# Two chains in the mixers: S5 moved behind RWKV and into its PSUM banks, RG-LRU left behind sparse attention

## The chip, the core and the metric

One core of a Trainium2 chip runs the whole program. The metric is the device time of one execution in microseconds (us), and lower is better. TensorE is called PE here, VectorE DVE, ScalarE ACT, GpSimd POOL, and SP is the queue that issues the weight transfers.

## What is computed

The program is a decoder trunk of two layers over 256 tokens, 1024 wide, in float32. In each layer the normalized input is projected once, and four causal token mixers, each 256 wide, work on parts of that projection. Their outputs are projected back to 1024, weighted by sigmoid gates and summed, and a mixture of experts follows.

```python
h = rmsnorm(x, mix_norm_g[l]) * (1.0 + scale1) + shift1
u, q, k, v, iq, ik, iw, rg_x, rg_g, rw_f = _split(h @ w_in[l], IN_WIDTHS)
o_s5 = s5_mixer(u, ...)          # diagonal complex state space scan, gelu, GLU
o_dsa = dsa_mixer(q, k, v, iq, ik, iw, positions)   # indexer, top 64 keys, attention
o_rg = rglru_mixer(rg_x, rg_g, ...)   # width 4 convolution, gates, real scan, gelu gate
o_rw = rwkv7_mixer(rw_f, ...)    # token shift, delta rule recurrence, group norm, bonus, gate
up = einsum('btnw,nwd->btnd', [o_s5, o_dsa, o_rg, o_rw], branch_w[l])
gates = sigmoid(h @ gate_w[l] + gate_b[l])
x = x + gate1 * ((gates * up).sum(branches) @ out_w[l])
x = x + gate2 * moe(rmsnorm(x, ffn_norm_g[l]) * (1.0 + scale2) + shift2)
```

## The kernel before, in words

The four mixers are Python generators. Each `yield` ends a piece of work, and a loop at the end of the program (L1741 to L1748) takes one piece from each chain in turn. The order of those pieces, and a scheduler behind it that keeps each engine's instructions in one queue, set what stands where. Nothing in that order depends on run time. Each engine works through its own queue in order.

The kernel before has two long chains. The first is `rwkv` (from L787): projections, the products of one chunk of 64 tokens with another, five levels of a triangular inverse (L944 to L957), a recurrence over four chunks (L963 to L1000), then a normalization of each head (L1003 to L1012, L1020) that has to be transposed back through PE (L1014). The second is `others` (L760): the token-major projection of attention, the three feature-major projections, the sparse attention `dsa` (from L1049), then `s5` (L1170), then `rglru` (L1243). In the first layer a third chain, `s5_tables` on POOL, makes the cosines and sines that S5 rotates with. In the second layer these tables were made beside the experts of the first.

Between the pieces the loop takes pieces of a filler (`fill`, L1291). It computes the 16 gate products of a layer (L640, three matmuls for each pair of tiles, because weights and inputs are split into a high and a low half by ACT L607 and DVE L608), the modulation vectors of later stages (`ada`, L474, whose weighted sums run on DVE at L495), and the merges of finished branches (`merge`, L1318). The plan string fixes their order; `b`, the merge of sparse attention, is the first merge, behind ten gate products. A merge whose branch is not finished gives its turn back, and nothing behind it starts. Pieces that are left when the chains have ended are worked off at once (L1752). The last two merges, of S5 and of RG-LRU, run as split products (L1334), and the output projection and the experts follow.

S5 works in eight steps of one group each. A step makes two products on PE (L1194), rotates them on DVE out of PSUM (L1198, L1199), adds halves on POOL (L1200, L1201), scans on DVE (L1203) and rotates back on DVE and POOL (L1204, L1205). After four steps 16 products (L1212) sum into one bank that S5 holds from its first step to its last. Then come the gelu (L1163 to L1167, a helper that RG-LRU uses too), and the GLU product (L1232).

The eight PSUM banks are three named `acc` (projections, gates, merges), two named `mx` and three named `rw`. Before the change S5, sparse attention, RG-LRU and the modulation vectors share `mx`; RWKV alone uses `rw` in the mixers.

```python
PSB = dict(acc=3, mx=2, rw=3)
FILL, SPARE = (2, 2, 2, 2, 1, 3, 3), 2        # filler pieces behind each chain's piece, by steps // 8
py = pt("mx", B2)                             # S5's sum, held
pbu = pt("mx", B2)                            # S5's products of one step
```

Of the kernel before, what the change touches and what calls it, by code (L numbers as in the profile page):

```python
# [28 lines left out]
KEEP, FREE0 = 1, 6  # L29
FILL, SPARE = (2, 2, 2, 2, 1, 3, 3), 2  # L30
XAT, MAT_AT = 3, 3
PLAN = "1311330100b0322d22ac"
PSB = dict(acc=3, mx=2, rw=3)
TM = (164, 256, 256, 256)
# [39 lines left out]
def bc(ap, shape):  # L74
    return ap.to_broadcast(list(shape))
# [71 lines left out]
def _emit(ctx, tc, I, out):  # L147
# [22 lines left out]
    def pt(tag, shape):  # L170
        uid[0] += 1
        return psp.tile(list(shape), F32, tag=tag, name=f"{tag}_{uid[0]}", bufs=PSB[tag])
# [3 lines left out]
    state = dict(next=0, wide=True, keep=FREE0)  # L176
# [98 lines left out]
    for l in range(L):  # L275
        c = ct(f"cols{l}", [P, NCOL])
# [480 lines left out]

    B2, C8 = [P, 2, T], [P, 8, 64]

    def others(l, m, tabs, brs):  # L760

        dp = {}
        yield from dsa_in(l, dp)
        u, X, gt = M.take(B2), M.take(B2), M.take(B2)
        for b, o in enumerate((u, X, gt)):
            S.activation(o, feat_mm(("fm", l, b), 2), AF.Copy)
            yield
        state["fill"] = True
        yield from dsa(l, dp, brs)
        while not tabs:  # L770
            yield
        yield from s5(l, u, m, tabs, brs)
        yield from rglru(l, X, gt, m, brs)


    def idb(j):
# [393 lines left out]
    def s5(l, u, m, tabs, brs):  # L1170
        cs, sn = tabs

        cre = m("s5_c_re").rearrange("p (j c) -> p j c", j=8)
        cim = m("s5_c_im").rearrange("p (j c) -> p j c", j=8)
        kr = bc(s5c[:, l, 0][:, :, None], [P, 8, 32])
        ki = bc(s5c[:, l, 1][:, :, None], [P, 8, 32])
        C, tm = M.take([P, 4, 8, 32]), M.take([P, 8, 32])
        G.tensor_tensor(C[:, 0], cre, kr, OP.mult)
        G.tensor_tensor(tm, cim, ki, OP.mult)
        G.tensor_tensor(C[:, 0], C[:, 0], tm, OP.subtract)  # L1180
        G.tensor_tensor(C[:, 1], cre, ki, OP.mult)
        G.tensor_tensor(tm, cim, kr, OP.mult)
        G.tensor_tensor(C[:, 1], C[:, 1], tm, OP.add)
        G.tensor_scalar(C[:, 2:4], C[:, 0:2], -1.0, None, op0=OP.mult)
        M.free(tm)
        b_re, b_im = m("s5_b_re"), m("s5_b_im")
        py = pt("mx", B2)
        for blk in range(2):
            ww = []
            for j in range(4 * blk, 4 * blk + 4):  # L1190
                q = slice(32 * (j % 4), 32 * (j % 4) + 32)
                pbu = pt("mx", B2)
                for i, bm in ((0, b_re), (1, b_im)):
                    PE.matmul(pbu[:, i], bm[q, P * blk:P * blk + P], u[q, blk, :], start=True, stop=True)  # L1194
                csb = bc(cs[:, j][:, None, :], B2)
                snb = bc(sn[:, j][:, None, :], B2)
                z, z2, w = (M.take(B2) for _ in range(3))
                V.tensor_tensor(z, pbu, csb, OP.mult)  # L1198
                V.tensor_tensor(z2, pbu, snb, OP.mult)  # L1199
                G.tensor_tensor(z[:, 0], z[:, 0], z2[:, 1], OP.add)  # L1200
                G.tensor_tensor(z[:, 1], z[:, 1], z2[:, 0], OP.subtract)  # L1201
                for i in range(2):
                    V.tensor_tensor_scan(w[:, i], bc(s5r[:, l, j:j + 1], [P, T]), z[:, i], 0.0, OP.mult, OP.add)  # L1203
                V.tensor_tensor(z, w, csb, OP.mult)  # L1204
                G.tensor_tensor(z2, w, snb, OP.mult)  # L1205
                M.free(w)
                ww.append((z, z2))
                yield

            for i, (ci, k, r) in enumerate(((0, 0, 0), (2, 1, 1), (3, 0, 1), (3, 1, 0))):  # L1210
                for j in range(4):
                    PE.matmul(py[32 * j:32 * j + 32, blk, :], C[:, ci, 4 * blk + j, :], ww[j][k][:, r],  # L1212
                              start=i == 0, stop=i == 3)
            for z in ww:
                M.free(*z)
            yield
        M.free(C)
        y = M.take(B2)
        for h in range(2):
            V.scalar_tensor_tensor(y[:, h], u[:, h], col(l, "s5_d", h), py[:, h], op0=OP.mult, op1=OP.add)  # L1220
        M.free(u)
        yield
        g2 = M.take(B2)
        gelu2(g2, y)
        M.free(y)
        hb = sm("s5hb", [P, 2])
        V.tensor_scalar(hb, col(l, "glu_b", 0, 2), 0.5, None, op0=OP.mult)
        gw = m("glu_w").rearrange("p (k c) -> p k c", k=2)
        pg = pt("mx", B2)
        for h in range(2):  # L1230
            for kt in range(2):
                PE.matmul(pg[:, h], gw[:, kt, P * h:P * h + P], g2[:, kt], start=kt == 0, stop=kt == 1)  # L1232
        o = M.take(B2)
        for h in range(2):
            S.activation(o[:, h], pg[:, h], AF.Tanh, scale=0.25, bias=hb[:, h:h + 1])
        V.scalar_tensor_tensor(o, o, 1.0, g2, op0=OP.add, op1=OP.mult)
        V.tensor_scalar(o, o, 0.25, None, op0=OP.mult)
        M.free(g2, cs, sn)
        brs[0] = o
        yield  # L1240
# [482 lines left out]
    for l in range(L):  # L1723
        mixers = ExitStack()
        if l == 0:
            mixers.enter_context(tc.issue_after(lead.ins))
        modT_halves(x, rs, mod[l, "scale", 0], mod[l, "shift", 0])
        if l == 0:
            prep()

        def m(name):
            o, n = MAT[name]
            return get(("mats", l))[:, o:o + n]

        brs, mix = [None] * 4, {}
        state["fill"], state["spare"] = False, SPARE
        tabs = tables[l]
        chains = [rwkv(l, m, brs), others(l, m, tabs, brs)] + ([] if tabs else [s5_tables(l, tabs)])
        fl = fill(l, brs, mix)
        steps = 0  # L1740
        while chains:  # L1741
            steps += 1
            for c in list(chains):
                if next(c, chains) is chains:
                    chains.remove(c)
                if state["fill"] and tabs:
                    for _ in range(FILL[min(steps // 8, 6)]):
                        next(fl, None)  # L1748
        mixers.close()
        state["spare"] = 0  # L1750
        state["wide"], state["keep"] = True, KEEP
        for _ in fl:  # L1752
            pass
        done(("mats", l))
        for dp in range(4):
            mix_halves(mix, dp)
        lg = out_proj(l, x)
        gate2, g2 = gate_rows(l, 1)
        oh, sid, wts, used, regi = route(l, lg)
        rs = experts(l, x, oh, sid, wts, used, regi, gate2, s5_tables(l + 1, tables[l + 1]) if l + 1 < L else ())  # L1760
        M.free(g2)
# [105 lines left out]
```

## Time and profile before

| | us |
|---|---|
| median of three runs | 1214.31 |
| lowest and highest | 1213.58, 1215.57 |
| the profiled execution, its own time | 1220.22 |
| its span, first to last instruction | 1218.4 |
| PE busy, DVE busy, ACT busy, POOL busy in that span | 1101.7, 746.6, 371.3, 230.3 |

The profiled execution took 5.9 us longer than the median, and 1.8 us of its time lie outside its span. Busy time of PE is to be read with care: the ends of matmuls are modelled, and one that is called 280 ns long can be followed by the next after 114 ns, so a PE that is busy all the time need not be at its rate. The table by stage and the times of single lines tell more than these sums.

### The profile page before, as it was taken

The page shows a single profiled execution, that of the slowest core. Times are in us where ns is not written, and L with a number is a line of the kernel's source. Part 1 is how long each engine was busy: PE and PEld are TensorE (multiplying, and loading weights), DVE is VectorE, ACT ScalarE, POOL GpSimd, SP SyncE. Part 2 cuts the span into 40 slices and gives each one's busy share as a digit, 9 for nine tenths or more (in the row PEclk, how much of TensorE's full clock was granted, in tenths as well). Part 3 has the DMA queues.
Part 4 walks back from the last instruction along what each step waited for, and adds up shares of the span by engine and source line. Part 5 has one row for each costly group of instructions (what it writes and reads, how often), then busy time and mean ns, then how long its engine had stood idle before and what let it go on. Part 6 is the DMA issues. An engine that isn't in the chain of part 4 may idle for free. (4 is left out here: it accounts for less than half of the span.)

```text
span 1218.4 us, 22986 instructions
## 1 busy us (share of the span) xinstructions
PE 1101.7 (90%) x9402; PEld 712.7 (58%) x9402; DVE 746.6 (61%) x1459; ACT 371.3 (30%) x663; POOL 230.3 (19%) x306
## 2 busy tenths in 40 slices
PE   4968998988989999999888999999898999999995
PEld 1867886866976333433238888987677743343331
DVE  5899995488777322434146899967987642243325
ACT  1643532422643111111026634433254311111112
POOL 0395211044140000009100031004524000000000
PEclk8998998998999999999898999999899999999998
DMA  8724786724565799998773467843155769999883
GB/s 359 280 99 164 287 302 223 307 105 172 208 235 215 259 421 420 421 420 361 316 288 105 172 244 290 299 175 139 42 201 224 294 228 411 420 422 420 363 360 159
DMA packets 47089, 329.84 MB, mean 271 GB/s; under 512 B 5992, under 2 KB 6120, under 8 KB 7552
## 3 DMA queue, kind: packets, MB, share of 16 engines
q1 hardware_dynamic: 45776, 327.47, 69.0%
q8 instruction: 79, 1.29, 0.4%
q10 hardware_dynamic: 1200, 0.79, 0.2%
q14 instruction: 34, 0.28, 0.1%
HBM read 327.19 MB, written 1.05 MB: 269 GB/s over the span
## 5 line engine op out<-in xcount | busy, mean ns | idle before, releaser
L640 PE MATMUL acc<-h_hi,whi 128*128 128x256 f32 x720 | 212.8, 296 | 0.0
L640 PE MATMUL acc<-h_hi,wlo 128*128 128x256 f32 x720 | 206.1, 286 | 4.9 <-DVE wlo L608 4.9
L640 PE MATMUL acc<-h_lo,whi 128*128 128x256 f32 x720 | 205.1, 285 | 1.0 <-DVE h_lo L608 1.0
L607 ACT ACTIVATE whi<-ring 128x1024 fp32r<-128x1024 f32 (+2 forms) x122 | 126.0, 1034 | 206.2 <-PE acc L640 127.1
L608 DVE TENSOR_TENSOR wlo<-ring,whi 128x1024 fp32r<-128x1024 f32 (+2 forms) x122 | 153.1, 1259 | 54.8 <-ACT whi L607 50.3
L640 PEld LDWEIGHTS acc<-h_hi,whi 128*128 128x128 f32 x720 | 139.3, 194 | 17.0 <-issue 8.5
L640 PEld LDWEIGHTS acc<-h_hi,wlo 128*128 128x128 f32 x720 | 139.3, 193 | 9.0 <-DVE wlo L608 6.9
L640 PEld LDWEIGHTS acc<-h_lo,whi 128*128 128x128 f32 x720 | 139.2, 193 | 4.7 <-issue 3.0
L1601 PE MATMUL rw<-page,page 128*32 (+1 forms) x736 | 92.3, 594 | 0.0
L495 DVE SCALAR_TENSOR_TENSOR page<-ring,csil,page 128x512 f32<-128x512 f32 x112 | 83.9, 786 | 0.0
L1601 PE MATMUL acc<-page,page 128*32 128x512 f32 (+1 forms) x688 | 83.0, 609 | 0.8 <-DVE page L1545 0.6
L1573 DVE TENSOR_TENSOR page<-page,acc 128x512 f32<-128x512 f32 x64 | 42.3, 684 | 54.8 <-PE acc L1572 54.7
L1623 PE MATMUL mx<-page,page 128*32 128x512 f32 (+1 forms) x560 | 65.7, 607 | 6.1 <-ACT page L1520 6.1
L1632 DVE SCALAR_TENSOR_TENSOR page<-mx,moslw,page 128x512 f32<-128x512 f32 x32 | 24.0, 751 | 75.3 <-PE mx L1623 73.7
L1545 DVE TENSOR_SCALAR page<-mx,scale,shift 128x256 f32<-128x256 f32 x32 | 17.4, 543 | 78.5 <-PE mx L1541 78.5
L607 ACT ACTIVATE wlo<-page 128x512 fp32r<-128x512 f32 x32 | 20.2, 631 | 129.7 <-DVE page L1632 120.7
L1543 ACT ACTIVATE page<-mx,shift,scale 128x256 f32<-128x256 f32 x32 | 18.1, 564 | 126.2 <-PE mx L1541 126.2
L1623 PE MATMUL mx<-ring,page 128*32 (+1 forms) x464 | 55.4, 614 | 0.7 <-ACT page L1520 0.7
L1601 PEld LDWEIGHTS rw<-page,page 128*32 128x32 f32 x736 | 24.4, 110 | 51.7 <-issue 49.0
L1572 PE MATMUL acc<-wlo,whi 128*128 128x512 f32 x128 | 43.0, 433 | 11.1 <-PEq L1611 5.7
L1343 POOL TENSOR_TENSOR page<-page,page 128x512 f32<-128x512 f32 x22 | 33.6, 1553 | 74.8 <-DVE page L1341 73.7
L1601 PEld LDWEIGHTS acc<-page,page 128*32 128x32 f32 x688 | 20.2, 112 | 44.3 <-issue 38.0
(523 smaller groups left out, 2125.1 us busy)
## 6 DMA issues: line engine op xcount, KB each, us to landing
page<-in_w SPq DMA_DIRECT2D x124, 1024.0 KB, 11.6
ring<-in_w SPq DMA_DIRECT2D x68, 1024.0 KB, 11.2
ring<-in_ada_w SPq DMA_DIRECT2D x45, 1024.0 KB, 5.5
ring<-in_gate_w SPq DMA_DIRECT2D x32, 1024.0 KB, 5.0
ring<-in_branch_w SPq DMA_DIRECT2D x8, 1024.0 KB, 4.9
ring<-in_w_rw SPq DMA_DIRECT2D x6, 1024.0 KB, 10.4
ring<-in_w_tm SPq DMA_DIRECT2D x6, 1024.0 KB, 4.8
ring<-in_w_fm SPq DMA_DIRECT2D x6, 1024.0 KB, 4.9
```

What stands on the lines that cost most here:

```text
L495: V.scalar_tensor_tensor(p[:, js], w[:, js], csil[:, kt, 0:1], p[:, js], op0=OP.mult, op1=OP.add)
L607: S.activation(hi, a, AF.Copy)
L608: V.tensor_tensor(lo, a, hi.bitcast(F32), OP.subtract)
L640: PE.matmul(p, w, x_, **f)
L1343: G.tensor_tensor(mix[dp], mix[dp], t, OP.add)
L1543: S.activation(xg[:, kt], p, AF.Identity, scale=sc[:, kt:kt + 1], bias=sh[:, kt:kt + 1])
L1545: V.tensor_scalar(xg[:, kt], p, sc[:, kt:kt + 1], sh[:, kt:kt + 1], op0=OP.mult, op1=OP.add)
L1572: state["pe"] = PE.matmul(p, oh[:, P * a:P * a + P], y[:, fs], start=y is yh, stop=y is yl)
L1573: V.tensor_tensor(x[:, a, fs], x[:, a, fs], p, OP.add)
L1601: PE.matmul(hh[f][32 * g:32 * g + 32, :], xg[:, kt, P * i + 32 * g:P * i + 32 * g + 32], w[:, ds(offs[g] + 512 * f, 512)], start=kt == 0, ...
L1623: PE.matmul(yp[f][32 * g:32 * g + 32, :], gT[:, ft, 32 * g:32 * g + 32], w[:, ds(offs[g] + 512 * f, 512)], start=ft == 0, stop=ft == 3)
L1632: V.scalar_tensor_tensor(t, yp[f], o["w"][:, i:i + 1], gate2[:, fs], op0=OP.mult, op1=OP.mult)
```

## The change

S5 leaves the second chain and follows RWKV in the first. Its three kinds of PSUM tiles move from `mx` to `rw`. The second chain ends with RG-LRU, directly behind sparse attention. And once the filler is running and two chains are left, every fourth step of the loop passes over the second chain, with the filler pieces that would have followed it.

```diff
+REST = 4
-    def others(l, m, tabs, brs):
+    def second_chain(l, m, brs, now):
...
         state["fill"] = True
+        now["u"] = u
         yield from dsa(l, dp, brs)
-        while not tabs:
-            yield
-        yield from s5(l, u, m, tabs, brs)
         yield from rglru(l, X, gt, m, brs)
+
+    def first_chain(l, m, tabs, brs, now):
+
+        yield from rwkv(l, m, brs)
+        yield
+        assert len(tabs) == 2
+        yield from s5(l, now["u"], m, tabs, brs)
...
-        py = pt("mx", B2)
+        py = pt("rw", B2)
...
-                pbu = pt("mx", B2)
+                pbu = pt("rw", B2)
...
-        pg = pt("mx", B2)
+        pg = pt("rw", B2)
...
-        chains = [rwkv(l, m, brs), others(l, m, tabs, brs)] + ([] if tabs else [s5_tables(l, tabs)])
+        now = {}
+        chains = [first_chain(l, m, tabs, brs, now), second_chain(l, m, brs, now)] + ([] if tabs else [s5_tables(l, tabs)])
...
-            for c in list(chains):
+            for i, c in enumerate(list(chains)):
+                if i == 1 and state["fill"] and len(chains) == 2 and steps % REST == 0:
+                    continue
                 if next(c, chains) is chains:
```

No instruction of the mixers is added or removed; they move. Three places show how. The line numbers after the change are larger by 1 in the helpers and by 6 in the mixers (L640 is L641 there, L1198 is L1204, L1271 is L1277).

DVE's queue in the first layer, where S5 begins. `rwmu`, `rwvar`, `rki`, `rkt` and `rwrs` belong to RWKV's normalization, `wlo` to a gate product, the rows with `mx` or `rw` on the right to S5's first rotations. Before:

```order
L608 TENSOR_TENSOR wlo_2884<-ring_70,whi_2883 128x1024
L1004 TENSOR_REDUCE rwmu_2814<-page_73 128x8
L1198 TENSOR_TENSOR page_81<-mx_2797,page_84 128x512
L1199 TENSOR_TENSOR page_75<-mx_2797,page_85 128x512
L1005 TENSOR_SCALAR rwmu_2814<-rwmu_2814 128x8
L1006 TENSOR_TENSOR page_73<-page_73,rwmu_2814 128x512
L1203 SCALAR_TENSOR_TENSOR page_82<-s5r,page_81 128x256 x2
L1198 TENSOR_TENSOR page_80<-mx_2845,page_84 128x512
```

With the change:

```order
L356 SCALAR_TENSOR_TENSOR rwrs_2673<-rkt_2681,rky_272_2690 128x8
L1018 TENSOR_TENSOR page_74<-page_74,rwrs_2673 128x512
L609 TENSOR_TENSOR wlo_2896<-ring_70,whi_2895 128x1024
L1026 TENSOR_TENSOR page_73<-page_73,page_76 128x512
L1204 TENSOR_TENSOR page_81<-rw_2754,page_84 128x512
L1027 TENSOR_TENSOR page_73<-page_73,page_75 128x512
L1205 TENSOR_TENSOR page_82<-rw_2754,page_85 128x512
L1204 TENSOR_TENSOR page_75<-rw_2790,page_84 128x512
```

S5's first rotation stood one row behind the start of RWKV's normalization and now stands behind nearly all of it.

PE's queue at the same place: L997 is RWKV's last product of a chunk, L784 turns its output, L1194 makes S5's products, L640 is a gate product, L1140 a transpose of attention's weights. Before:

```order
L994 MATMUL rw_2762<-page_73,page_77 64x64
L996 MATMUL rw_2762<-page_73,page_76 64x64
L997 MATMUL rw_2762<-page_76,page_77 64x64
L640 MATMUL acc_2778<-h_hi,whi_2779 128x256
L640 MATMUL acc_2778<-h_lo,whi_2779 128x256
L640 MATMUL acc_2778<-h_hi,wlo_2780 128x256
...
L1194 MATMUL mx_2797<-page_82,page_79 128x256 x2
```

With the change, the end of the piece that stands between them now:

```order
L1146 MATMUL mx_2812<-identr,page_73 128x128
L641 MATMUL acc_2849<-h_lo,whi_2850 128x256
L641 MATMUL acc_2849<-h_hi,wlo_2851 128x256
L1146 MATMUL mx_2812<-identr,page_73 128x128
L641 MATMUL acc_2849<-h_hi,whi_2850 128x256
L790 MATMUL rw_2702<-identr,page_74 64x64 x16
L1200 MATMUL rw_2754<-page_82,page_79 128x256 x2
```

Between RWKV's last product and S5's first there stood 6 gate matmuls; now 79 stand there, with 16 turns of RWKV and 5 matmuls of attention. Ahead of S5's first product the layer has 757 gate and feature matmuls of L640 in place of 750.

DVE's queue in the first layer where S5 and RG-LRU end (L1271 is RG-LRU's reciprocal, L1236 S5's last product but one). Before:

```order
L1236 SCALAR_TENSOR_TENSOR page_73<-page_73,page_82 128x512
L1237 TENSOR_SCALAR page_73<-page_73 128x512
L608 TENSOR_TENSOR wlo_3259<-ring_70,whi_3258 128x1024
L1270 TENSOR_SCALAR page_75<-page_82 128x512
L1271 RECIPROCAL page_75<-page_75 128x512
L1272 TENSOR_SCALAR page_82<-page_82 128x512
L1274 SCALAR_TENSOR_TENSOR page_73<-page_74,page_73 128x512
```

With the change:

```order
L1276 TENSOR_SCALAR page_75<-page_74 128x512
L1277 RECIPROCAL page_75<-page_75 128x512
L1204 TENSOR_TENSOR page_83<-rw_3083,page_84 128x512
L1205 TENSOR_TENSOR page_82<-rw_3083,page_85 128x512
L609 TENSOR_TENSOR wlo_3133<-ring_68,whi_3132 128x1024
L1209 SCALAR_TENSOR_TENSOR page_81<-s5r,page_83 128x256 x2
L609 TENSOR_TENSOR wlo_3181<-ring_69,whi_3180 128x1024
L1210 TENSOR_TENSOR page_83<-page_81,page_84 128x512
```

RG-LRU's tail stood behind S5's end and now stands inside S5's last step.

## Rows read from the trace of the kernel before

**Rows 1.** Busy time by stage (start:end us, length, engines, clock, DMA share, GB/s).

```profile
128.00:190.00 62.00, 58.85 (x894) 52.54 (x896) 59.87 (x109) 24.82 (x55) 7.93 (x7) 1.00 0.80 291
...
206.00:249.70 43.70, 43.70 (x477) 34.96 (x473) 22.76 (x50) 19.02 (x42) 4.08 (x6) 1.00 0.70 264
249.70:306.10 56.40, 46.98 (x314) 34.98 (x314) 52.57 (x78) 13.20 (x21) 25.58 (x24) 0.94 0.38 144
306.10:340.00 33.90, 32.68 (x234) 29.24 (x234) 25.07 (x29) 20.68 (x33) 5.47 (x4) 1.00 0.54 199
...
836.00:895.80 59.80, 51.66 (x351) 41.07 (x349) 56.23 (x82) 16.43 (x25) 27.70 (x25) 0.89 0.38 140
895.80:923.10 27.30, 24.17 (x155) 19.66 (x155) 20.56 (x23) 15.09 (x26) 5.62 (x4) 1.00 0.35 120
...
399.00:640.00 241.00, 226.60 (x1813) 83.57 (x1812) 77.03 (x133) 32.99 (x56) 35.84 (x74) 0.97 0.91 367
```

**Rows 2.** Single lines, first layer (shortest/median/longest ns, first to last start us).

```profile
L997 PE MATMUL rw<-page,page x32: 218/218/218, 209.6 to 247.4; 64*64 64x64 f32 x32
...
L1198 DVE TENSOR_TENSOR page<-mx,page x8: 657/660/694, 249.7 to 289.5; 128x512 f32<-128x512 f32 x8
...
L1232 PE MATMUL mx<-page,page x8: 379/379/454, 306.1 to 307.7; 128*128 128x256 f32 x8
...
L1334 PE MATMUL acc<-h_hi,whi x32: 276/276/419, 340.0 to 353.7; 128*128 128x256 f32 x32
```

**Rows 3.** The same lines, second layer, and RG-LRU's last.

```profile
L997 PE MATMUL rw<-page,page x32: 218/218/218, 798.7 to 834.8; 64*64 64x64 f32 x32
...
L1198 DVE TENSOR_TENSOR page<-mx,page x8: 657/676/681, 836.0 to 877.9; 128x512 f32<-128x512 f32 x8
...
L1232 PE MATMUL mx<-page,page x8: 379/379/454, 895.8 to 897.4; 128*128 128x256 f32 x8
...
L1284 DVE SCALAR_TENSOR_TENSOR page<-page,page x1: 691/691/691, 913.4 to 913.4; 128x512 f32<-128x512 f32 x1
```

**Rows 4.** Timeline of PE, 43 gate matmuls lie from the first to the second row.

```profile
184.56 0.28 PE L640 MATMUL acc<-h_hi,whi 128*128 128x256 f32 x1
...
189.44 0.28 PE L640 MATMUL acc<-h_lo,whi 128*128 128x256 f32 x1
```

**Rows 5.** DVE groups, 249.7 to 330 us (count, busy us, mean ns, idle before).

```profile
L608 DVE TENSOR_TENSOR wlo<-ring,whi 128x1024 fp32r<-128x1024 f32 x10 | 12.6, 1264 | 0.0
...
L1271 DVE RECIPROCAL page<-page 128x512 f32<-128x512 f32 x1 | 3.4, 3353 | 0.0
...
L1277 DVE TENSOR_SCALAR page<-page 128x512 f32<-128x512 f32 x1 | 1.5, 1516 | 0.0
...
L1280 DVE TENSOR_TENSOR_SCAN page<-page,page 128x256 f32<-128x256 f32 x2 | 1.3, 669 | 0.0
L353 DVE SCALAR_TENSOR_TENSOR rkt<-rkt,rwvar 128x8 f32<-128x8 f32 x3 | 1.1, 359 | 0.0
L1020 DVE TENSOR_TENSOR page<-page,page 128x512 f32<-128x512 f32 x1 | 0.9, 907 | 0.0
...
L1275 DVE TENSOR_TENSOR page<-page,page 128x512 f32<-128x512 f32 x1 | 0.7, 685 | 0.0
...
L1272 DVE TENSOR_SCALAR page<-page 128x512 f32<-128x512 f32 x1 | 0.4, 364 | 0.0
```

**Rows 6.** PE groups, 249.7 to 340 us, same columns.

```profile
L1259 PE MATMUL mx<-page,page 64*64 64x256 f32 x16 | 2.2, 389 | 0.0
...
L520 PE MATMUL mx<-page,ones_f 1*128 1x512 f32 x4 | 1.1, 640 | 0.0
```

**Rows 7.** S5's scan over both layers (columns as in rows 2).

```profile
L1203 DVE TENSOR_TENSOR_SCAN page<-s5r,page x32: 658/679/1212, 252.4 to 883.4; 128x256 f32<-128x256 f32 x32
```

**Rows 8.** The longest wait of PE in S5, 249.7 to 306.1 us (total, times, longest).

```profile
PEld mx L1212 <- POOL page L1205: 7.5, 4, 2.2
```

## The prediction, made before the changed kernel was run

> **What bounds the kernel now.** I read the stages first, then where single lines stand in them, then the costs. The change moves work between the start of RWKV's recurrence and the split merges, so I cut each layer there. Stage I ends with S5's first rotation on DVE (249.7 and 836.0 us), stage II with S5's GLU product on PE (306.1 and 895.8), stage III with the first split merge (340.0 in the first layer; 923.1, where the second layer's stage III ends) [rows 1 to 3]. What follows is the same in both kernels, and the reader is to see that the three stages have different limits. From 128 to 190 us DVE is busy 59.87 of 62.00 us: DVE binds. From 206 to 249.7 us DVE has only 22.76 of 43.70 us to do, and PE holds matmuls all the time: the recurrence and the gate products on PE bind. Stage II is DVE's again, 52.57 of 56.40 us in the first layer and 56.23 of 59.80 in the second, with PE idle for 9.4 and 8.1 us. In stage III of the first layer PE binds, 32.68 of 33.90 us, with DVE at 25.07 [rows 1]. In the second layer PE is idle for 3.1 of 27.30 us, since RG-LRU's last instruction on DVE ends only at 914.1 (913.4 and its 0.691) and a half of a gate's weight waits behind it [rows 1, 3].
>
> So a chain's DVE work costs nothing before 249.7 us, costs its full length in stage II, and nothing again in the first layer's stage III. PE's work costs its length in stages I and III and nothing in stage II. The change is a set of moves across these borders.
>
> **The change part by part.** A gate matmul takes PE 4.88 / 43 = 0.1135 us when they follow each other [rows 4]. All counts are from the queues' order.
>
> Stage I. S5's first rotation was free to run right after the start of RWKV's normalization; now it stands behind it. The normalization is five instructions of 512 elements (0.68 each, as the 0.685 of L1275, one of them 0.907), three of 0.36, and twelve more of 8 elements, which I put at 0.15 to 0.8: some 7.6 us [rows 5]. With two gate or attention sums, a reduction and the gate halves that stand between (three at 1.264 in the first layer, two in the second), DVE has 13.9 us from the normalization's start to S5's first rotation in the first layer and 11.9 in the second, where 0.7 stood before. Against that, RWKV's last product, at 247.4 and 834.8 us [rows 2, 3], comes earlier. In the first layer 79 gate matmuls stand between it and S5's first product where 6 stood, and 7 more of them stand ahead of S5 in all, so at least 66 x 0.1135 = 7.5 us of PE have gone behind it. With the attention that has gone there too (its last transposes and outputs, RWKV's turns) I count 10.8, which at the pace of this stretch (some 1.1 us of time for each) is 11.9. S5's rotation then comes at 247.4 - 11.9 + 1.4 + 13.9 + 0.5 (a square on ACT) = 251.3, or 1.6 us later; with gates alone, at 255.7, or 6.0 later. In the second layer 42 gate matmuls have gone behind, 4.8 us, with the rest 8.9, in time about 10.0: 834.8 - 10.0 + 0.6 + 11.9 + 0.5 = 837.8, or 1.8 later, and 7 later with gates alone. I take the early ends, +1.6 and +1.8, since the attention's moved products are real.
>
> Stage II, DVE. RWKV's normalization leaves it: -7.6 us, in the second layer -6.7, since L1020 stays in it. RG-LRU's tail enters: a reciprocal of 3.353, a scaling of 1.516, two scans 1.34, and six more of 0.364 to 0.685, together 9.7 us [rows 5]. In the first layer one gelu more (two instructions as L1275, 1.4) and two halves of gate weights (2.5) enter, in the second two halves leave. That makes +13.6 - 7.6 = **+6.0 us** in the first layer and 9.7 - 6.7 - 2.5 = **+0.5 us** in the second, all of it on the path as long as DVE binds. Sparse attention's end, which enters too, brings DVE nothing here: its additions and reductions stand ahead of S5. The products it brings to PE (2 us) lie in PE's 9.4 us of idle time.
>
> Stage III, PE. From S5's GLU product to the first split merge there stand 139 gate matmuls in both layers, where 173 and 96 stood: -3.9 and +4.9 us. RG-LRU's gate products (2.2) and two rows of a modulation vector (1.1) have gone ahead of it in both [rows 6]. First layer: 33.9 - 3.9 - 3.3 = 26.7, **-7.2 us**. The second layer's queue holds the same matmuls there, and DVE's backlog is gone, so it takes the same 26.7 in place of 27.3: **-0.6 us**. Fully summed over PE alone it would be 27.3 + 1.6 = 28.9, the bound on the other side, +1.6.
>
> The other parts come to nothing. REST takes a quarter of the second chain's turns, and with them filler; what is passed over stands later in the same queues and is counted above. The merge of attention stops the filler until attention has ended, later than before; that is why fewer gate matmuls stand in the second layer's S5, counted too. The `rw` banks give S5 two for its products where `mx` left one; they would help PE, whose waits in stage II hold up nothing that binds. POOL and ACT get the same instructions, and SP issues the same transfers in the same order, out of pages that come free at other times; the experts' weights come at 367 GB/s with the DMA engines busy 0.91 of their stage [rows 1], and that stage starts its prefetch when the mixers end, so it moves with them, one for one.
>
> Sum: first layer 1.6 + 6.0 - 7.2 = +0.4; second 1.8 + 0.5 - 0.6 = +1.7. Together +2 us, on the profiled execution's 1220.2, which stands 5.9 above the median; on the median 1214.3 + 2 = **1216 us**. About 0.2%, or 2.4 us, is what a measurement of this kernel can tell from no change, so this is no change.
>
> **The rivals.** *PE's waits mattered.* PE waits inside stage II for S5's own instructions, 7.5 us of them for POOL's last rotation [rows 8], and a blocked PE delays gate products and with them the halves that DVE has. With two banks for S5 and a second chain beside it, DVE would have no gap. Its gaps are the price: 56.4 - 52.6 = 3.8 and 59.8 - 56.2 = 3.6 us [rows 1], so 1216 - 7.4 = 1209 us, and 1206 if stage I hides the normalization too. For it: S5 alone beside the filler leaves DVE little choice. Against: 93% is nearly full.
>
> *RWKV's tail becomes the wait.* This ends slower. In one chain, S5 cannot begin before RWKV's recurrence and its normalization have run through, and the recurrence, with less filler between, is nearer to its own latency. It decides from the point where RWKV's last product is less than about 12 us earlier than now. At the far ends of stage I it costs 6.0 + 7.0 in place of 3.4: 1216 + 9.6 = 1226 us. For it: chunks of the recurrence already take (247.4 - 209.6) / 3 = 12.6 us from first to last start [rows 2], while only some 8.4 us of PE's work per chunk remain. Against: DVE is half idle there, so nothing queues ahead of the chain.
>
> *DVE and POOL in each other's way.* S5's scans last 658 ns at the shortest and 1212 at the longest, with a median of 679 [rows 7], and POOL is busy 25.58 us of stage II [rows 1]. RG-LRU's tail ran with POOL nearly still and would now run beside S5's POOL work. If its two-input instructions (about 5 us a layer with the convolution) were doubled, as the longest scan is, that is +10 us: 1226. But POOL's time is the same and can block DVE only once, so I give it little. The Trainium skill, in "SBUF — State Buffer", section "Who interferes with whom", says that a DVE instruction with two SBUF inputs and a GpSimd one that reads SBUF exclude each other for the whole instruction. The spread of the scans agrees with that.
>
> *The queues bind as before.* If the scheduler's moves are absorbed wherever they fall, the time is 1214.
>
> **How the numbers follow.** The forecast's own case has 0.48, with its parts open to about 5 us either way: 0.09 faster, 0.22 within, 0.17 slower. PE's waits have 0.27 (0.25 faster, 0.02 within). RWKV's tail has 0.15 and the collision with POOL 0.05, all slower. The unmoved case has 0.05, within. Together 0.34 faster, 0.29 within, 0.37 slower. The range reaches from 1205, the first rival with stage I hidden, to 1227, the two slow ones.
>
> **What would show it.** Right: S5's first rotation at 251 and 838 us, its GLU product near 314 and 898, the first split merge near 340 and 925, stage II at over 0.92 DVE with PE idle for more than 10 us, and RG-LRU's last instruction ahead of the GLU product. Wrong: DVE idle by more than 6 us in stage II, S5's rotation later than 254 and 841, or a stage III longer than 29 us. Scans with a mean above the 0.9 us of now would speak for the collision.

## The result and the profile after

The changed kernel takes 1230.53 us (median of four runs, 1225.83 to 1233.39) beside 1214.94 for the kernel before on the same chip (median of four, 1213.58 to 1225.81). The ratio is 1.0104, with a 95% interval of 1.0062 to 1.0146: slower by 12.6 us where no change was forecast, and above the upper end of the range.

The table by stage of the changed kernel, cut as in [rows 1] (start:end us, length, busy us of PE, its weight loads, DVE, ACT and POOL, granted clock, DMA share, GB/s). The first row is the start of the recurrence, the others are stages II and III of the two layers:

```profile
206.00:245.80 39.80, 39.03 (x417) 30.68 (x409) 27.19 (x65) 17.29 (x39) 7.70 (x9) 1.00 0.68 265
245.80:314.80 69.00, 58.06 (x342) 43.21 (x341) 61.13 (x75) 20.97 (x33) 27.06 (x24) 0.85 0.30 107
314.80:342.30 27.50, 25.25 (x182) 24.01 (x180) 13.04 (x14) 13.07 (x21) 5.11 (x4) 1.00 0.48 158
837.00:902.00 65.00, 52.92 (x316) 37.88 (x314) 58.45 (x73) 18.87 (x30) 26.06 (x24) 0.82 0.25 91
902.00:929.30 27.30, 25.05 (x180) 23.81 (x179) 13.05 (x14) 12.29 (x20) 5.11 (x4) 1.00 0.60 213
```

Single lines of the changed kernel in the first layer, then in the second (shortest/median/longest ns, first to last start us): RWKV's last products, S5's rotations, its GLU product, the split merges, RG-LRU's last instruction. They answer to [rows 2, 3]:

```profile
L1003 PE MATMUL rw<-page,page x32: 218/218/218, 195.9 to 230.0; 64*64 64x64 f32 x32
L1204 DVE TENSOR_TENSOR page<-rw,page x8: 630/676/684, 245.8 to 292.6; 128x512 f32<-128x512 f32 x8
L1238 PE MATMUL rw<-page,page x8: 377/379/379, 314.9 to 316.4; 128*128 128x256 f32 x8
L1340 PE MATMUL acc<-h_hi,whi x32: 276/276/387, 342.3 to 353.9; 128*128 128x256 f32 x32
L1290 DVE SCALAR_TENSOR_TENSOR page<-page,page x1: 693/693/693, 308.3 to 308.3; 128x512 f32<-128x512 f32 x1
L1204 DVE TENSOR_TENSOR page<-rw,page x8: 629/676/690, 837.0 to 882.1; 128x512 f32<-128x512 f32 x8
L1238 PE MATMUL rw<-page,page x8: 379/379/483, 902.0 to 903.6; 128*128 128x256 f32 x8
L1340 PE MATMUL acc<-h_hi,whi x32: 276/276/385, 929.3 to 941.5; 128*128 128x256 f32 x32
```

Between the two profiles the 5.7 us of the spans split so: S5's start 3.9 earlier, stage II of the first layer 12.6 longer (69.0 for 56.4, by chance the same figure as the loss of the runs), stage III 6.4 shorter (27.5 for 33.9), the way to the second layer's S5 1.3 shorter, stage II there 5.2 longer (65.0 for 59.8), stage III 27.3 as before, the rest 0.5 shorter. All of the loss between the profiles lies in S5's stage.

The runs lost more than the profiles show. The two profiled executions lie on opposite sides of their medians: before's, 1220.22 us, 5.3 above, and the changed kernel's, 1225.83 us, 4.7 below and the lowest of four. Part of this can be seen. In the profile of before PE had a stretch at 1.2 GHz ahead of the recurrence, and the changed kernel had none. The two rows of that stretch, of before and then of the changed kernel:

```profile
190.00:206.00 16.00, 13.85 (x84) 7.91 (x76) 5.98 (x11) 4.05 (x8) 1.89 (x4) 0.79 0.53 197
```

```profile
190.00:206.00 16.00, 15.95 (x167) 12.07 (x170) 4.77 (x11) 5.27 (x11) 0.00 (x0) 1.00 0.79 310
```

In the eight profiles of kernels below that keep the old order up to S5, RWKV's last product starts at 239.1 to 246.9 us; before's 247.4 is the latest of the nine, their median 242.8. S5's first rotation stands 2.2 to 2.3 behind it, at about 245.1. The changed kernel's 245.8 is thus 0.7 us later, not 3.9 earlier, and with 0.7 in place of -3.9 the stages give +10.3 us, near the 12.6 of the runs.

DVE in stage II of the first layer by groups (count | busy us, mean ns | idle before, releaser), of before and then of the changed kernel: S5's scans and its product that rotates back.

```profile
L1203 DVE TENSOR_TENSOR_SCAN page<-s5r,page 128x256 f32<-128x256 f32 x16 | 14.0, 900 | 2.1 <-POOL page L1200 2.1
L1204 DVE TENSOR_TENSOR page<-page,page 128x512 f32<-128x512 f32 x8 | 10.3, 1287 | 0.0
```

```profile
L1209 DVE TENSOR_TENSOR_SCAN page<-s5r,page 128x256 f32<-128x256 f32 x16 | 14.3, 929 | 3.3 <-POOL page L1206 3.3
L1210 DVE TENSOR_TENSOR page<-page,page 128x512 f32<-128x512 f32 x8 | 13.1, 1636 | 0.0
```

### The profile page after: what moved, and what is told of

Read it like the earlier page. It is cut to its first block, busy times and chain, and to the rows that moved or that the text cites. A ratio compares the mean times of both kernels' runs of the same rounds, so it can differ in the third digit from the quotient of the medians.

```text
span 1224.1 us, 22968 instructions
## 1 busy us (share of the span) xinstructions
PE 1100.0 (90%) x9402; PEld 714.3 (58%) x9402; DVE 746.3 (61%) x1459; ACT 371.2 (30%) x663; POOL 237.9 (19%) x306
## 5 line engine op out<-in xcount | busy, mean ns | idle before, releaser
L641 PE MATMUL acc<-h_hi,whi 128*128 128x256 f32 x720 | 214.0, 297 | 0.0
L641 PE MATMUL acc<-h_hi,wlo 128*128 128x256 f32 x720 | 206.6, 287 | 7.4 <-DVE wlo L609 7.3
L641 PE MATMUL acc<-h_lo,whi 128*128 128x256 f32 x720 | 204.9, 285 | 0.9 <-DVE h_lo L609 0.9
L609 DVE TENSOR_TENSOR wlo<-ring,whi 128x1024 fp32r<-128x1024 f32 (+2 forms) x120 | 149.2, 1247 | 64.6 <-ACT whi L608 64.5
L641 PEld LDWEIGHTS acc<-h_hi,whi 128*128 128x128 f32 x720 | 139.8, 194 | 13.9 <-issue 10.2
L641 PEld LDWEIGHTS acc<-h_hi,wlo 128*128 128x128 f32 x720 | 139.3, 194 | 13.7 <-DVE wlo L609 10.7
L641 PEld LDWEIGHTS acc<-h_lo,whi 128*128 128x128 f32 x720 | 139.0, 193 | 2.4 <-DVE h_lo L609 1.6
L1607 PE MATMUL acc<-page,page 128*32 128x512 f32 (+1 forms) x672 | 79.9, 602 | 0.8 <-DVE page L1551 0.6
L1629 PE MATMUL mx<-ring,page 128*32 x464 | 54.8, 610 | 3.1 <-ACT page L1526 3.1
L1515 DVE SCALAR_TENSOR_TENSOR page<-page,rw 128x512 f32<-128x512 f32 x8 | 5.5, 686 | 64.5 <-ACT page L1514 64.5
```

The costliest lines, as they stand in the source:

```text
L609: V.tensor_tensor(lo, a, hi.bitcast(F32), OP.subtract)
L641: PE.matmul(p, w, x_, **f)
L1607: PE.matmul(hh[f][32 * g:32 * g + 32, :], xg[:, kt, P * i + 32 * g:P * i + 32 * g + 32], w[:, ds(offs[g] + 512 * f, 512)], start=kt == 0, ...
L1629: PE.matmul(yp[f][32 * g:32 * g + 32, :], gT[:, ft, 32 * g:32 * g + 32], w[:, ds(offs[g] + 512 * f, 512)], start=ft == 0, stop=ft == 3)
```

## The experiments

Each was timed in five rounds against the kernel before on its own chip. Theory 1: the lost time lies in DVE's work in S5's stage. Theory 2: PE's clock there. Theory 3: the banks. Theory 4: DVE and POOL block each other.

| run | what differs | ratio | interval |
|---|---|---|---|
| the change | | 1.0104 | 1.0062 to 1.0146 |
| e1_no_rest | change, no turn passed over | 1.0072 | 1.0043 to 1.0101 |
| e2_banks_only | before, S5 in rw | 1.0134 | 1.0089 to 1.0178 |
| e3_chains_mx | change, S5 in mx | 1.0130 | 1.0094 to 1.0166 |
| e4_rg_last | change, RG-LRU behind S5 | 1.0034 | 1.0011 to 1.0056 |
| e5_after_warm | change, dummy matmuls | 1.0170 | 1.0146 to 1.0193 |
| e6_banks_warm | e2, dummy matmuls | 1.0234 | 1.0212 to 1.0255 |
| e7_after_rot_dve | change, back rotation on DVE | 1.0039 | 1.0018 to 1.0061 |
| e8_before_rot_dve | before, back rotation on DVE | 0.9965 | 0.9948 to 0.9982 |
| e9_rg_last_rot_dve | e4, back rotation on DVE | 1.0017 | 0.9993 to 1.0041 |
| e10_before_s5_dve | before, S5's steps on DVE | 0.9878 | 0.9843 to 0.9912 |
| e13_after_s5_dve | change, S5's steps on DVE | 0.9961 | 0.9942 to 0.9981 |
| e14_rg_last_s5_dve | e4, S5's steps on DVE | 1.0013 | 0.9991 to 1.0034 |
| e15_sum_bank_only | before, S5's sum in rw | 1.0023 | 1.0003 to 1.0044 |
| e16_s5_dve_sum_bank | e10, S5's sum in rw | 0.9988 | 0.9970 to 1.0006 |
| e17_s5_dve_fill | e10, more filler in steps 32 to 39 | 0.9884 | 0.9857 to 0.9911 |
| e18_s5_dve_again | e10 once more | 0.9882 | 0.9853 to 0.9910 |

**REST away.**

```diff
-REST = 4
+REST = 10 ** 9
```

> The change, but the second chain is never passed over. By the queues' order RG-LRU then ends 40 to 45 us of DVE work ahead of S5's gelu, and DVE's work in S5's stage (stage II) is 50.5 and 48.4 us in place of the change's 64.2 and 62.8, while DVE has 5.5 and 9 us more between RWKV's normalization and S5's first rotation. Theory 1 (the time went into DVE's work in stage II: RG-LRU's tail and gate halves, on the path): stage II falls from 69.0 and 65.0 us to 55 and 53, S5's start comes 4 to 8 us later than in the change, the split merges 5 to 9 us earlier in each layer, ratio to the kernel before 0.992 to 1.002. Theory 2 (TensorE at half its clock during S5 is what costs): S5 has even fewer gate products beside it (144 to 174), the granted clock of stage II stays at or below the change's 0.82 to 0.85, and the ratio stays at 1.008 or more.

Stage II fell nearly as theory 1 said, to 57.4 and 54.5 us, but S5 started at 261.4, 15.6 us later, not 4 to 8, and the ratio, 1.0072, missed the 0.992 to 1.002 of theory 1. In the stretch between RWKV's last product and S5's first rotation DVE, whose queue the rotation ends, is busy for 15.13 of 16.40 us, and PE, as modelled, for 16.35:

```profile
245.00:261.40 16.40, 16.35 (x135) 13.47 (x133) 15.13 (x30) 9.79 (x19) 0.00 (x0) 1.00 0.46 184
```

RG-LRU's tail and two merges were now ahead of S5: most of what stage II saved was paid there. At 1.0072 the interval overlaps the change's; REST is not shown to matter.

**RG-LRU behind S5.**

```diff
-        now["u"] = u
+        now.update(u=u, X=X, gt=gt)
...
-        yield from rglru(l, X, gt, m, brs)
...
         yield from s5(l, now["u"], m, tabs, brs)
+        yield from rglru(l, now["X"], now["gt"], m, brs)
```

> The change with RG-LRU put behind S5 in the first chain, so that S5 still follows RWKV but RG-LRU's work is out of S5's stage: DVE's work of stage II is 52.9 and 51.4 us (64.2 and 62.8), TensorE's from S5's GLU product to the split merges 30 and 31 (24.4 both). Theory 1: stage II 56 to 59 and 54 to 57 us, the next stage 33 to 35 us, the split merges 3 to 6 us earlier than in the change in each layer, ratio 1.000 to 1.005. Theory 2 (half clock in S5): the gate products beside S5 are fewer (157 and 120 for 184 and 149), so the clock in stage II stays below 0.85 and the ratio at 1.008 or more.

As theory 1 had it, but for the second layer's stage II, put at 54 to 57 us. Stage II is 58.3 and 58.5 us (10.7 and 6.5 less), stage III 32.6 and 33.1, and the ratio falls by 0.0070, or 8.5 of the 12.6 us, though the clock in stage II stayed at 0.85 and 0.75. Stage II of both layers:

```profile
245.50:303.80 58.30, 49.02 (x303) 37.56 (x302) 50.90 (x65) 15.36 (x24) 26.13 (x24) 0.85 0.31 109
...
831.90:890.40 58.50, 48.09 (x267) 34.14 (x267) 48.39 (x62) 12.22 (x20) 24.37 (x24) 0.75 0.19 73
```

DVE is busy only 50.90 and 48.39 us of them, so DVE's work alone does not make these 58 us. DVE waits there for POOL's additions (2.8 and 3.7 us), for ACT's halves of gate weights (3.2 and 1.2) and, in the second layer, for PE's products. That S5's own chain through PE, DVE and POOL is nearly that long is argued from this; no run shows that chain by itself.

**One instruction out of RG-LRU's tail**, in the change and in the kernel before. Without the reciprocal other values reach the router and other experts run, so the whole time says nothing; the mixers' stages can be read, in the second layer by their lengths.

```diff
-        V.reciprocal(Rr, Rr)
```

> The change without RG-LRU's reciprocal (3.356 us of DVE a layer, which now stands in S5's last step); its result is then not the reciprocal but the sum itself. Theory 1 (DVE's work in stage II is on the path in full): both stages II fall by 3 to 4 us, 6.7 us in all, ratio 1.0104 - 0.0055 = 1.003 to 1.007. Rival (S5's chain of steps through PE, DVE and POOL binds, DVE only looks full): under 2 us in all, ratio 1.008 to 1.011.

> The kernel before without the same reciprocal, which stands there in stage III. Theory 1: nothing in the first layer, where TensorE binds in that stage, and 0 to 3.4 us in the second, where TensorE waits for RG-LRU's end: ratio 0.997 to 1.000. Rival (DVE's work counts wherever it lies between RWKV and the split merges): 6.7 us, ratio 0.993 to 0.996.

Stages II of the change without it, and stage III of the first layer of before without it:

```profile
246.10:308.90 62.80, 53.74 (x339) 40.31 (x337) 58.16 (x74) 21.63 (x33) 26.67 (x24) 0.89 0.33 115
2240.70:2302.50 61.80, 51.45 (x310) 37.49 (x311) 55.35 (x72) 18.99 (x30) 25.62 (x24) 0.81 0.24 88
```

```profile
307.10:341.50 34.40, 32.80 (x233) 29.09 (x233) 22.81 (x28) 20.50 (x33) 6.04 (x4) 1.00 0.51 188
```

An instruction of 3.36 us took 6.2 and 3.2 us of stage II with it, none of stage III of the first layer (34.4 for 33.9) and 1.8 us of the second's (25.5 for 27.3). These are single profiles, and 6.2 is more than the instruction can be; the clock rose beside it, from 0.85 to 0.89. Theory 1 holds: the reciprocal was free where it stood in the first layer, cost about half of its length there in the second, and costs about its length or more where it stands now.

**PE's clock.** Dummy matmuls that nobody reads, 80 a layer, in S5: six behind each step, four ahead of each pass of the sum.

```diff
+                keep_busy(6)
...
+                keep_busy(4)
```

> The change with dummy matmuls (128x256, into an mx bank that nobody reads) in S5: 6 behind each of its eight steps and 4 ahead of each of the eight passes of its sum, 80 a layer. Theory 2 (TensorE's clock: it waits in S5's stage, is granted 1.2 GHz there, and the time follows; over the runs of the first experiment 1218 us went with a mean clock of 0.958 and 1230 with 0.944): the clock in stage II rises from 0.82 to 0.85 to over 0.92, the mean of the runs from about 0.951 to over 0.960, and the ratio falls from 1.0104 to 1.000 to 1.006. Theory 1 (DVE's work alone): the clock may rise, but the ratio stays at 1.009 to 1.015, since the dummies only add to TensorE's queue.

> The kernel before with S5 in the rw banks, and the same 80 dummy matmuls a layer. The banks alone gave 1.0134 at a mean clock of 0.941 to 0.952. Theory 2: the clock rises to 0.955 or more, stage II falls from 61.3 and 61.6 us to 55 to 59, the ratio to 1.000 to 1.006. Theory 3 (S5's products and RWKV's last turns wait for each other's banks, whatever the clock): stage II keeps its 61 us and the ratio stays at 1.012 or more.

In e5 the clock of stage II rose to 0.91 and 0.90, but the stage became 4.2 us longer in both layers, and the ratio rose to 1.0170. In e6, where the clock of stage II is 0.84 and 0.83 for the 0.83 and 0.78 of e2, the time rose too. As theory 2 stated it, that the ratio falls when the clock is raised so, it failed. That the clock costs nothing is not shown, since the dummies (a median of 273 ns each) took PE's time themselves.

```profile
244.30:317.50 73.20, 63.76 (x426) 46.51 (x426) 62.54 (x76) 22.97 (x36) 26.80 (x24) 0.91 0.27 97
839.20:908.40 69.20, 59.17 (x379) 41.86 (x380) 60.71 (x74) 21.16 (x35) 26.10 (x24) 0.90 0.27 96
```

Other rows show that the clock is a part of the time. e10 and e18, below, are one kernel twice. In stage II of the first layer DVE has the same work in both, the clock differs, and so does the length, by 3.3 us. In the slower one DVE waits 3.9 us for PE's products, in the other 0.7:

```profile
243.50:300.20 56.70, 52.41 (x325) 39.19 (x326) 52.00 (x102) 14.14 (x22) 0.00 (x0) 0.82 0.40 147
```

```profile
241.30:294.70 53.40, 46.94 (x326) 35.61 (x326) 52.01 (x103) 14.23 (x22) 0.00 (x0) 0.94 0.43 157
```

In the kernel before and the change the clock of stage II was 0.94 and 0.89, then 0.85 and 0.82. S5's last sum shows it, of before at a granted clock of 1.00 and of the change at 0.53; in the change DVE has nothing to do for 2.2 us of it:

```profile
L1212 PE MATMUL mx<-page,page x20: 376/379/403, 298.6 to 300.1; 128*32 128x256 f32 x20
```

```profile
L1218 PE MATMUL rw<-page,page x22: 506/634/634, 300.3 to 303.1; 128*32 128x256 f32 x22
```

How much of the kernel's 12.6 us goes with the clock is open. Over some 250 runs, each against the mean of its own kernel, a mean clock lower by 0.01 goes with 5.5 us more; the change's runs have a median of 0.952, those of before beside the experiments 0.958 to 0.959. That would be some 4 us, an estimate from a correlation, since a stage that makes PE wait longer may lower the clock as well.

**The banks alone, the chains alone.** S5's `py`, `pbu` and `pg` in `rw` in the kernel before, and in `mx` in the change.

> The kernel before with S5's three PSUM tiles in the rw banks and nothing else: 5 of 6 counts of its queues in the first layer stay the same, in the second layer 43 gate matmuls pass from S5's stage to the one behind it. Theory 1: no change, ratio 0.998 to 1.002, stage II of the first layer 55 to 57 us. Theory 3 (the banks themselves are what slows S5, since its products now come early and leave TensorE waiting, or the reverse, they help): ratio above 1.005 or below 0.995.

> The change with S5's three PSUM tiles left in mx, so chains and REST alone. By the order DVE's work of stage II is 73.5 and 67.4 us (64.2 and 62.8 in the change), since S5's start moves ahead of more of RWKV's normalization and of attention's end. Theory 1: stage II takes 75 to 80 and 69 to 74 us, S5's start 6 to 9 us earlier, so the split merges within 4 us of the change's, ratio 1.005 to 1.02. Theory 3 (banks): at 1.000 or below if the rw banks are what slows, above 1.02 if they help.

Here theory 1 missed: the banks alone cost 1.3%. PE's queue in that kernel, S5's products (L1194) and RWKV's turns (L784), and S5's products in the kernel before (start us, length):

```profile
241.74 1.13 PE L1194 MATMUL rw<-page,page 32*128 32x256 f32 x4
244.37 1.12 PE L1194 MATMUL rw<-page,page 32*128 32x256 f32 x4
261.57 1.15 PE L784 MATMUL rw<-identr,page 64*64 64x64 f32 x32
262.64 1.14 PE L1194 MATMUL rw<-page,page 32*128 32x256 f32 x8
```

```profile
248.51 1.13 PE L1194 MATMUL mx<-page,page 32*128 32x256 f32 x4
251.14 1.12 PE L1194 MATMUL mx<-page,page 32*128 32x256 f32 x4
253.76 1.13 PE L1194 MATMUL mx<-page,page 32*128 32x256 f32 x4
```

With one of three `rw` banks held, S5's third product waits until RWKV's turns have had theirs, 21 us behind the first. To settle this, the sum alone was put in `rw`:

> The kernel before with S5's sum alone in an rw bank, its products and the GLU product in mx, so that S5 has two banks for its products and none of them is one that RWKV's last turns must have first. In the run with all three in rw, S5's third product waited behind those turns until 262.6 us, 20 us behind its first rotation; in the kernel before it started at 257.4, 7.8 behind. Theory 5 (that wait is what the banks cost): S5's third product comes at most 9 us behind the first rotation, stage II of the first layer 54 to 58 us, ratio 0.995 to 1.003. Rival (a held bank of rw, or the second layer's 43 gate matmuls that pass behind S5's stage as they did there): 1.008 to 1.014.

(The expectation gives the fourth product's time, 257.4, as the third's, which is 253.76.) The third product then starts at 250.02, 4.1 us behind the first rotation as in the kernel before, stage II is 57.9, and the ratio 1.0023. So S5's products in `rw`, with that wait, were most of what the banks cost in the old order. In the change S5 stands behind RWKV's turns and doesn't meet it: `mx` or `rw`, 1.0130 or 1.0104, can't be told apart. There the chains alone cost what the change costs, within the intervals; stage II took 77.5 us, within theory 1's 75 to 80, and 75.2 in the second layer, above its 69 to 74.

**POOL.** The back rotation, and then the two additions of each step too, given to DVE:

```diff
-                G.tensor_tensor(z2, w, snb, OP.mult)
+                V.tensor_tensor(z2, w, snb, OP.mult)
```

> The change with POOL's product of S5's back rotation (L1211, eight of 128x512 a layer) given to DVE. Theory 4 (DVE and POOL block each other: DVE's own product beside it takes 1636 ns on average where 680 is its length alone, and TensorE waits 7.5 us for POOL's): DVE's product falls to 700 to 900 ns, both together take at most 12 us a layer where DVE's alone took 13.1 and 11.8, stage II falls by 3 to 8 us, ratio 1.000 to 1.006. Theory 1 without it (POOL's work is out of DVE's way): eight more products of 0.68 us, 5.4 us a layer on the binding engine, ratio 1.015 to 1.02.

> The kernel before with the same product given to DVE. Theory 4: DVE's product takes 680 to 800 ns in place of 1287 and 1422 (a median of 1.4 us), so the sixteen cost what the eight cost, and TensorE's waits for POOL go: ratio 0.993 to 1.001. Without it: 5.4 us a layer more on DVE in a stage that it binds, ratio 1.006 to 1.01.

> The kernel before with all of S5's steps on DVE: the back rotation and the two additions of 128x256 of each step. Theory 4 (POOL blocks DVE): S5's scans fall from a mean of 900 and 933 ns to 660 to 700, 3.8 us a layer; the sixteen additions cost DVE 16 x 0.35 to 0.4 = 5.6 to 6.4 us a layer; the waits of DVE for POOL's additions (2.1 and 2.5 us) end and the chain of a step is shorter by two POOL instructions of 1.0 and 0.75 us: ratio 0.993 to 0.999. Theory 1 alone (DVE's work in stage II is the time): from the 0.9965 with the rotation on DVE up by 2 to 3 us a layer, 1.000 to 1.003.

> The change with all of S5's steps on DVE, as the kernel before was run with them (0.9878). Theory A (RG-LRU's DVE work in S5's stage is a cost of its own, beside POOL's blocking): the distance between the two orders with the rotation alone on DVE, 1.0039 - 0.9965 = 0.0074, stays: 0.993 to 0.997, stage II still 6 to 9 us longer than with the old order. Theory B (the change cost what it did because RG-LRU's instructions met POOL's; without POOL they fit): 0.986 to 0.991, within the interval of the old order, stage II at 60 us or less in the first layer.

Theory 4 holds: more work on the engine that binds makes both orders faster, by more than was expected of e10: 0.9965 and 0.9878 for the old, 1.0039 and 0.9961 for the new. (Stage II of e7 fell by 3.8 and 1.2 us, in the second layer less than the 3 to 8 put.) How much of it is the blocking was not taken apart: with POOL's instructions gone a step's chain is shorter too, and the scheduler gives other orders. S5's groups on DVE in the kernel before with all steps on DVE, when run again:

```profile
L1203 DVE TENSOR_TENSOR_SCAN page<-s5r,page 128x256 f32<-128x256 f32 x16 | 10.3, 675 | 0.0
L1205 DVE TENSOR_TENSOR page<-page,page 128x512 f32<-128x512 f32 x8 | 5.5, 682 | 0.0
L1204 DVE TENSOR_TENSOR page<-page,page 128x512 f32<-128x512 f32 x8 | 5.4, 681 | 0.0
L1200 DVE TENSOR_TENSOR page<-page,page 128x256 f32<-128x256 f32 x6 | 2.5, 418 | 0.0
```

But the distance between the two orders stays: 1.04% with POOL as it was, 0.74% with the rotation on DVE, 0.83% with all on DVE (intervals that overlap). By these POOL's blocking is a cost of both orders and not the main reason for the loss; the intervals leave it a part. Theory A's numbers for e13 came out, stage II is 6.7 and 6.6 us longer than in e10 (63.4 for 56.7, 62.8 for 56.2), and theory B falls.

**RG-LRU behind S5, without POOL.**

> RG-LRU behind S5 in the first chain (1.0034 alone) and S5's back rotation on DVE. Theory A (three costs that add: S5's later start, RG-LRU's DVE work in S5's stage, POOL blocking DVE): the rotation gives what it gave in the kernel before, 0.35%, so 0.998 to 1.002, with stage II at 55 to 58 us and S5's start still 3 to 5 us later behind RWKV's last product than its normalization's start would allow. Theory B (the blocking is what RG-LRU's presence costs, and with RG-LRU gone there is nothing left to take): 1.002 to 1.005.

> S5 behind RWKV, RG-LRU behind S5, all of S5 on DVE. With POOL's instructions it stood 0.34% behind the kernel before, with the rotation on DVE 0.52% behind the old order with the same. Theory A (what is left is S5's later start, 3 to 5 us a layer less what stage III gives): 0.990 to 0.994. Rival (the two orders differ by POOL alone): 0.985 to 0.989.

e9 lies on the border of its two theories, and e14 missed both on the slow side. Taking RG-LRU out of S5's stage gave 0.70% with POOL, 0.22% with the rotation on DVE, and with all of S5 on DVE it lost 0.52%. In e14 stages II and III are 56.3 + 33.2 and 53.0 + 33.1 us, in e13 63.4 + 24.8 and 62.8 + 22.3: what leaves stage II comes back in III. So the price of RG-LRU in S5's stage depends on POOL's part in it; why it turns around is not settled.

**What stands behind S5.**

> All of S5's steps on DVE in the old order, and its sum in an rw bank: both parts together, as a version that may beat both kernels. If the sum's bank is worth nothing or a little by itself: 0.984 to 0.989. If the gate matmuls that pass behind S5's stage in the second layer cost: 0.990 to 0.998.

> The old order with all of S5's steps on DVE, and two filler pieces instead of one behind each chain's piece in steps 32 to 39. By the order 42 more gate matmuls then stand ahead of S5 in the first layer and 96 instead of 161 between its GLU product and the split merge; three halves and three merges more lie in stage II. The second layer's counts change little (one more half before S5's gelu). If gate products behind S5 cost their length and those before it are hidden: the first layer's stage III falls from 33.3 to 20 to 24 us, stages I and II grow by 5 to 9, and the ratio is 2 to 6 us below that of the same kernel with one piece. If the work only changes places: the same ratio within 0.002.

> The kernel of the run with 0.9878 once more, on the chip of the run beside it. If that gain was the kernel's: 0.984 to 0.992. If its six runs lay low by chance: 0.993 to 0.998, the half percent that the rotation alone gave and a little more.

e18 repeats the gain: 1201.96 beside 1217.03 us, 0.9882. It beats both kernels by over 1%. e16 loses it again, 1.1%, with 45 gate matmuls passed from stage II of the second layer to III, which takes 36.6 us there for 22.0 in e10. In e15 the same edit passed 42 (stage III 36.3 for 27.3) and went with 0.23%; what such a passing costs is not settled. e17 took 65 out of the first layer's stage III, which fell from 33.3 to 24.5, and gained nothing: S5 started at 251.2 for 243.5. There the work only changed places.

## Why the prediction was wrong

**What bounds it.** Right in part: the reciprocal counts in stage II, where DVE was said to bind, and not in III of the first layer, where PE was (e11, e12). But DVE's work is not all that sets stage II: e10 and e18 have the same and differ by 3.3 us.

**Stage I.** Forecast +1.6 and +1.8. Against the median of the nine profiles the first was +0.7; the second was -1.3, within what such profiles differ by (493.5 to 499.1 us from the first split merge to S5 in the old order). The normalization did become a wait of its own: S5 was put 15.8 and 13.0 us behind RWKV's last product and came 15.8 and 15.9 behind. But PE's work had left the recurrence for it, and the last product came earlier than put, at 230.0 and 821.2 for 235.5 and 824.8.

**Stage III.** Forecast 26.7 in both layers, measured 27.5 and 27.3; the count of 139 gate matmuls carried.

**Stage II, the step that failed.** I put +6.0 and +0.5 us of DVE and left DVE's gaps and the lengths of its instructions as they were. Measured: +12.6 and +5.2. DVE's busy time grew by 8.6 and 2.2, 2.6 and 1.7 more than put. In the first layer the work that moved came to some 5.4 of the 6.0 put (an estimate: the time that each instruction adds to DVE's busy time, summed). S5's own instructions took about 3.2 more, most of it in the rotation back, 13.1 for 10.3 us, that POOL blocks longer. The rest are gaps: 69.00 - 61.13 = 7.87 for 3.83, and 65.00 - 58.45 = 6.55 for 3.57. In the first layer they are waits for POOL's additions (3.3 for 2.1 us), 2.2 ahead of L1226, which reads the sum that PE makes at half its clock, 0.7 for ACT, and 1.6 at the end, where PE has gate products ahead of the GLU product. The prediction said itself that gaps over 6 us would prove it wrong. Its fault was to read 0.93 busy as one limit: with 51 and 48 us of DVE work the stage still took 58 (e4). In the first four steps DVE waited 1.7 us for POOL's additions, for 0.6 in the kernel before, where RWKV's short instructions stood between; RG-LRU's tail comes in a block late in the stage and leaves these holes. In the changed kernel, DVE ahead of two scans early in S5:

```profile
258.12 1.78 DVE L1209 TENSOR_TENSOR_SCAN page<-s5r,page 128x256 f32<-128x256 f32 x2 [0.24 <-POOL page L1206]
...
262.40 1.77 DVE L1209 TENSOR_TENSOR_SCAN page<-s5r,page 128x256 f32<-128x256 f32 x2 [0.61 <-POOL page L1206]
```

That the normalization filled holes is read from the traces, and is about 1 of the stage's 12.6 us; no run took it alone out of S5's stage. How the rest of the loss divides between RG-LRU's place, POOL and the clock stays open: taking RG-LRU out of the stage gave back 8.5 us with POOL's work as it was, and nothing with all of S5 on DVE (e14).

**The rivals.** PE's waits (1209): the gain did not come; the gaps grew. (With stage I hidden it comes to 1216 - 7.4 - 3.4 = 1205, not 1206.) RWKV's tail exposed (1226): the time came near, but not for its reason, since S5 did not start later than 254. DVE and POOL in each other's way (1226): the mechanism is there, and I gave it 0.05; POOL's part of S5 on DVE was worth 1.2% in the old order. By the central values it is a third of the loss or less, since the orders still differ by 0.74 and 0.83% with less of POOL's work; the intervals leave more open. REST and the banks: without the one or the other the change's time moved by less than the intervals can tell (1.0072, 1.0130), as put; in the old order the banks cost 1.3%.

## What to carry to other kernels

An engine that is busy 93% of a stage need not be its only limit: before work is moved into such a stage, look at the chain that runs through it, at the clock that PE has there, and at whether the work that leaves had filled its holes. Work that is free behind one engine's limit can be paid in full behind another's, so price each instruction by the stage where it will stand. Where a second engine's instructions lengthen those of the binding one, try giving it their work: here DVE's eight products back took 10.3 us in the first layer beside POOL's eight, and all sixteen took DVE 10.8 alone (e8). And take a profile twice before a stage's length is explained: one kernel's stage differed by 3.3 us between two.

## What the runs showed of the hardware

DVE's product of two operands in SBUF takes 0.68 us alone and up to 1.78 beside POOL's rotation; with POOL's work gone all eight take 681 ns on average, and the scans 675 for 900. S5's first rotations, with one operand in PSUM, kept 657 to 694 ns beside the same POOL work [rows 2]. The Trainium skill, in "SBUF — State Buffer", section "Who interferes with whom", states that a DVE instruction with two SBUF inputs contends with a GpSimd one that reads SBUF, and that one with at most one SBUF input, outside the two-port modes, does not; the runs agree with it, by the 1.78 us of the one and the 0.69 of the other. Giving S5's POOL work to DVE made this kernel 1.2% faster, with a shorter chain and the scheduler's new order in it.

Runs of one kernel go with PE's granted clock: in e1 the fastest, 1218 us, had a mean of 0.958 and the slowest, 1230, had 0.946. S5's last sum took 379 ns a product and 1.5 us from first to last at full clock, 634 ns and 2.8 us at about half.
